# A hybrid decoder layer on one core: row statistics ahead of the first q chunk's low parts on VectorE, and the transposes of the local branch's keys one slot later

## The chip, the cores and the metric

The kernel runs on one core of one Trainium2 chip. The metric is the device time of one execution in microseconds, as a median of several runs. Beside it stands one profiled execution, whose trace gives every number of the stages below. TensorE, VectorE, ScalarE, GpSimd and SyncE (which issues most loads) each have their own queue of instructions, work through it in order, and wait for each other by semaphores.

## The reference: what is computed

One decoder layer on x of 256 rows and 1024 columns, all in float32:

```
h    = rmsnorm(x, norm1_g)
proj = h @ w_in      -> q | k,v of 3 branches | 24 branch gates | q,k,v of MoBA | 2 merge gates
y_nsa  = compressed + selected-block + sliding-window attention, gated, 8 heads in 2 key groups
y_moba = block attention, 8 heads (one block of 256 rows: causal attention)
x = x + (sig(g_A) * (y_nsa @ w_up_nsa) + sig(g_B) * (y_moba @ w_up_moba)) @ w_out
x = x + relu(rmsnorm(x, norm2_g) @ w_ff1)^2 @ w_ff2
out = rmsnorm(x, norm_f_g)
```

With 256 rows every block is selected and the window of 512 covers all rows, so the second and third branch of the first mixer are plain causal attention over their own keys. The keys of the third, the sliding window, are the "local branch's keys" of the title (`kwT` in the code). The compressed branch turns blocks of 32 keys into one each, by a small network.

## The kernel before, in words

**Two halves of a number.** TensorE multiplies in a format with fewer bits than float32, so every weight and every activation is split into a high part and a low part, and a product is three matmuls: high by high, low by high, high by low (`mm3`, lines 219 to 222). The high part of a weight chunk is a copy on ScalarE (`whi`, L106), the low part a subtraction on VectorE (`wlo`, L108); both are in `split`, which takes a chunk in two or four pieces.

**Chunks and slots.** The weights are cut into 60 chunks of mostly 1 MB, in the order of their use: kva and kvb twice in turn (chunks 0 to 3), q (4, 5), qm (6, 7), km (8, 9), vm (10, 11), then the merge gates and the later layers. `load(c)` issues the transfer of chunk c on SyncE's queue. Raw, high and low tiles have three buffers each. One chunk's matmuls are a slot. While slot c runs, ScalarE and VectorE split chunk c + 2 or so, and SyncE loads chunk c + 5, as soon as the low parts that read the same raw buffer are done.

**An order written by hand.** `at(pos, f, ...)` notes a step at a position of the slot, from 0 to 1. `run_slot` then writes the slot's matmuls one by one and puts each step in front of the first matmul whose index divided by their number is at or above its position; steps of equal position keep their order. A slot here has 24 matmuls, so 0.1 means ahead of the fourth, 0.15 ahead of the fifth. Position decides only the order in each engine's queue; when a step runs is left to the semaphores.

**The first norm.** x comes in transposed, and the projection starts on x times the norm's gain at once, without the row factor. ScalarE squares x (`row_squares`), VectorE adds the squares up (`row_sums`, L186), and `row_norm` (from line 188) finishes the statistic: four small matmuls with a tile of ones sum over the partitions into a PSUM tile, VectorE scales the result into `stat` (L192), and GpSimd raises it to the power -0.5 (`rstd`, L193) and halves it (L194). The row factor `rstd` is applied when a projection leaves PSUM, by the scale of ScalarE's copy: `evac_tm` (L275 for the compressed branch's keys and values, `kcd`; L278 for the rest). So nothing of the projection can leave PSUM before `rstd` is there.

**The compressed branch.** `cmp_gather` (L345, L353) transposes `kcd` by four matmuls for the keys and, in its second call, four for the values, and VectorE writes them into `kE`. `cmp_mlp1`, `cmp_gelu` and `cmp_mlp2` run the network; `hid` (L365) and `bdk` (L384) are its first and its last key result.

**Keys and queries.** `transp_k` (L328) transposes a tile of 128 key columns by two matmuls, and `split_evac` takes them out as a high part, the first 128 columns in float32 (ScalarE, L315, L316) and a low part (VectorE, L317). `transp_heads` (L298) does the same for four heads of a query. All these use two PSUM banks in turn, `tp` and `yb`: each new tile takes the bank of the tile before the last, and waits until that has been read. `cmp_mlp2` takes both; the bank of its first tile, which `bdk` reads, goes to the local keys, and the next but one use of it is the second call of `transp_heads` for q in slot 6.

**The steps around the change.** Slots 2 to 6 as they stand before:

```
elif c == 2:
    for k in range(2):
        at(0.9, split, 4, k, 2, "l")
    at(0.91, load, 7)
else:
    at(0.15, row_norm)
    for t in range(2):
        at(0.2, evac_tm, "kva", t, first[t], 384)
    for k in range(2):
        at(0.7, split, 5, k, 2, "h")
    at(0.82, cmp_gather, 0)
```

In slot 5 the local keys' `transp_k` stands at 0.85, behind `cmp_mlp2` at 0.6; the second q evacuation is at 1.0. In slot 6 ScalarE's high parts of chunk 8 stand at 0.0 and 0.45, VectorE's low parts of it at 0.3 and 0.46, and the two `transp_heads` of q at 0.4 and 0.5. The keys are first read in slot 9.

Of the kernel before, what the change touches and what calls it, by code (L numbers as in the profile page):

```python
# [39 lines left out]
def hybrid_layer(ctx: ExitStack, tc: tile.TileContext, gxd, w, w1c, small, const, gf, out):  # L40
# [26 lines left out]
    def acc_tile():  # L67
        return next_bank("acc")
# [130 lines left out]
    def at(pos, f, *a):  # L199
        ev.append((pos, f, a))  # L200

    def run_slot(mms):
        n = len(mms)
        es = sorted(ev, key=lambda e: e[0])
        ev.clear()
        j = 0
        for i, m in enumerate(mms):
            while j < len(es) and es[j][0] <= i / n:
                es[j][1](*es[j][2])
                j += 1  # L210
            m()
        while j < len(es):
            es[j][1](*es[j][2])
            j += 1
# [9 lines left out]
    def xstat(c, n, accs, kts):  # L224

        r = []
        h, l = hi[c], lo[c]
        order = [(t, k) for t in range(2) for k in range(4)]
        if c < 3:
            order.sort(key=lambda e: e[1])  # L230
        for t, k in order:
            kt = kts[k]
            if True:
                lh, ll = (a[:, kt, t * 128:(t + 1) * 128] for a in (hTh, hTl))
                r += mm3(accs[t][:, :n], lh, ll, h[:, k * n:(k + 1) * n],
                         l[:, k * n:(k + 1) * n], kt == 0, kt == 7)
        return r
# [11 lines left out]
    def split_events(c, hs, ls):  # L249
        for i in range(2):  # L250
            at(hs[i], split, c + 2, i, 2, "h")
        for i in range(2):
            if ls[i] <= 1:
                at(ls[i], split, c + 2, i, 2, "l")
        if ls[1] <= 1:
            at(max(ls) + 0.05, load, c + 5)

    def std_events(c):
        if 9 <= c < 20 and c % 2:
            split_events(c, (0.0, 0.06), (0.09, 0.46))  # L260
        elif 9 <= c < 20:
            split_events(c, (0.0, 0.45), (0.3, 0.8))
        else:
            split_events(c, (0.0, 0.45), (0.3, 0.46))
# [4 lines left out]
    kvb = ap_.tile([128, 2, 408], F32, name="kvb")  # L269
# [49 lines left out]
    def qk_tiles(name, n, q):  # L319
        m = 128 if q else 256  # L320
        return (ap_.tile([128, n, 128], F32, name=name + "0"),
                ap_.tile([128, n, m], F32R, name=name + "h"),
                ap_.tile([128, n, m], F32R, name=name + "l"))
# [76 lines left out]
    ksT, kwT = (qk_tiles(n, 1, False) for n in ("ks", "kw"))  # L400
# [137 lines left out]
    def unit_events(s):  # L538
        d = (s - 9) // 2
        if not 9 <= s <= 21:  # L540
            return
        if s % 2 == 0:
            at(0.1, d_norm, d)
            at(0.78, d_trans, d)
            return
        if d < 6:
            at(0.1, d_scores, d)
        if d > 0:
            at(0.1, d_pv, d - 1)
        if d < 6:  # L550
            at(0.11, d_max, d)
            at(0.2 if s > 12 else 0.5, d_exp, d, 0)
            at(0.22 if s > 12 else 0.52, d_exp, d, 1)
        if d > 0:
            at(0.12, d_yevac, d - 1)
# [17 lines left out]
    for c in range(4):  # L573
        if c == 0:
            at(0.6, load, 5)
            at(0.6, nc.sync.dma_start, w1, w1c)
        elif c == 1:
            for k in range(2):
                at(0.5, split, 3, k, 4)
            at(0.5, row_sums, 0, 4, 2)  # L580
            at(0.5, row_sums, 0, 1, 1)
            for k in range(2, 4):
                at(0.5, split, 3, k, 4)
            at(0.51, load, 6)
            for k in range(2):
                at(0.6, split, 4, k, 2, "h")
        elif c == 2:
            for k in range(2):
                at(0.9, split, 4, k, 2, "l")
            at(0.91, load, 7)  # L590
        else:
            at(0.15, row_norm)
            for t in range(2):
                at(0.2, evac_tm, "kva", t, first[t], 384)
            for k in range(2):
                at(0.7, split, 5, k, 2, "h")
            at(0.82, cmp_gather, 0)
        accs = (first, second)[c % 2]
        run_slot(xstat(c, (384, 408)[c % 2], accs, range(2 * c - 2 * (c % 2), 2 * c - 2 * (c % 2) + 4)))
    groups = [("q", C_Q, 512), ("qm", C_QM, 512), ("km", C_KM, 512), ("vm", C_VM, 512)]  # L600
    for sec, c0, n in groups:
        if sec in ("q", "qm", "km"):
            tm[sec] = ap_.tile([128, 2, 512], F32, name="qtm", bufs=2)
        if sec == "q":
            accs = [ps_e.tile([128, 512], F32, name=f"{sec}acc{t}") for t in range(2)]
        else:
            accs = [acc_tile(), acc_tile()]
        for i in range(2):
            c = c0 + i
            if c == 4:  # L610
                for t in range(2):
                    at(0.0, evac_tm, "kvb", t, second[t], 408)
                at(0.05, cmp_gather, 1)
                at(0.1, split, 5, 0, 2, "l")
                at(0.2, rope, kva, 2)
                at(0.3, split, 5, 1, 2, "l")
                at(0.35, load, 8)
                split_events(c, (0.5, 0.55), (0.8, 0.9))
                at(0.7, cmp_mlp1)
                at(0.92, cmp_gelu)  # L620
            else:
                std_events(c)
            unit_events(c)
            if c == 5:
                at(0.05, gate_evac)
                at(0.1, transp_k, kva, ksT)
                at(0.1, rope, kvb[:, :, 0:128], 2)
                at(0.6, cmp_mlp2)
                at(0.85, transp_k, kvb[:, :, 0:128], kwT)
            if c == 6:  # L630
                at(0.4, transp_heads, tm["q"], qT, 0)
                at(0.5, transp_heads, tm["q"], qT, 1)
                at(0.6, rope, tm["q"], 8)
            if c == 7:
                at(0.1, cmp_scores)
                at(0.3, cmp_softmax)
                at(0.4, transp_heads, tm["q"], qrT, 0)
                at(0.55, transp_heads, tm["q"], qrT, 1)
            if c == 8:
                at(0.35, cmp_probs_t)  # L640
                at(0.3, rope, tm["qm"], 8)
            if c == 9:
                at(0.3, transp_heads, tm["qm"], qmT, 0)
                at(0.45, transp_heads, tm["qm"], qmT, 1)
            if c == 10:
                at(0.5, rope, tm["km"], 8)
            if c == 11:
                turn["tp"] = ["tp"]
                at(0.02, transp_heads, tm["km"], kmT, 0, False)
                at(0.48, transp_heads, tm["km"], kmT, 1, False)  # L650
            if i == 1:
                at(0.5, evac_tm, sec, 0, accs[0], n)
                at(1.0, evac_tm, sec, 1, accs[1], n)
            run_slot(xstat(c, n, accs, range(4 * i, 4 * i + 4)))
# [11 lines left out]
    for g in range(4):  # L666
        accs = [acc_tile(), acc_tile()]
        for i in range(2):
            c = C_GM + 2 * g + i
# [40 lines left out]
    for sec, c0, kind, evac in (("upn", C_UPN, "n", upn_evac), ("upm", C_UPM, "m", upm_evac)):  # L710
        for i in range(2):
            c = c0 + i
# [89 lines left out]
    for i in range(4):  # L802
        c = C_WOUT + i
# [46 lines left out]
    for i in range(16):  # L850
        c = C_FF1 + i
# [177 lines left out]
```

## Time and profile before

| | |
|---|---|
| median of 3 runs | 384.33 us (384.25 to 385.54) |
| profiled execution | 383.04 us |
| its span, first to last instruction | 381.3 us |
| TensorE busy | 370.3 us (97%) |
| VectorE busy | 254.4 us (67%) |
| ScalarE busy | 205.6 us (54%) |
| GpSimd busy | 4.2 us (1%), 15 instructions |
| granted TensorE clock, mean | 0.995 |

How it is read: PE is TensorE's matmuls and PEld its weight loads, DVE is VectorE, ACT is ScalarE, POOL is GpSimd, SP is SyncE. Times in the trace are microseconds from the first instruction. L with a number is a line of the kernel. `tp<-ident,kcd` is an instruction that writes `tp` and reads `ident` and `kcd`; "x4" merges four in a row, whose sizes may differ. A bracket behind a row gives how long the engine had been idle before it and what ended that. Matmuls are pipelined and their ends are modelled, so two of them overlap in the rows, and what one costs is read from the step between starts. Times between a load's issue and its landing are in the view of the transfers. The share of TensorE is high nearly everywhere: of 40 equal slices of the span, its busy share is 80% or more in all but the last.

### The profile page before, as it was taken

What the parts mean: (1) busy time and instruction counts of PE and PEld (TensorE: products, weight loads), DVE (VectorE), ACT (ScalarE), POOL (GpSimd) and SP (SyncE); (2) the same over time, 40 slices, a digit from 0 to 9 for tenths busy, and PEclk for the clock granted to TensorE, in tenths of its full rate; (3) what the DMA queues carried; (4) which work ended last, traced back from release to release, by engine and by line L of the source; (5) the groups of instructions that cost most, each with busy time, mean ns of one, the idle gap of its engine ahead of it and who ended that gap; (6) DMA issues with size and microseconds to landing.
All of it is one profiled execution on the core that took longest, in us unless ns stands there. A gap on an engine that the chain in (4) does not pass through costs nothing.

```text
span 381.3 us, 5936 instructions
## 1 busy us (share of the span) xinstructions
PE 370.3 (97%) x2406; PEld 323.9 (85%) x2406; DVE 254.4 (67%) x397; ACT 205.6 (54%) x360; POOL 4.2 (1%) x15
## 2 busy tenths in 40 slices
PE   8989899999999999999999999999999999999993
PEld 6977778877888787778999999999998888888883
DVE  3868687897867869766868666766676254334435
ACT  5975455847747667344455646565556454433412
POOL 2000000000000000000000000000000000000000
PEclk9999999999999999999999999999999999999998
DMA  7995436332433325450675545654565545644003
GB/s 259 372 385 191 166 110 222 110 112 111 160 149 136 110 112 193 156 203 0 237 261 219 195 159 203 222 194 162 198 222 192 187 175 217 220 166 166 1 2 111
DMA packets 10972, 66.38 MB, mean 174 GB/s; under 512 B 1216, under 2 KB 2752, under 8 KB 3648
## 3 DMA queue, kind: packets, MB, share of 16 engines
q1 hardware_dynamic: 10512, 65.21, 47.0%
q10 hardware_dynamic: 432, 0.79, 0.6%
q8 instruction: 19, 0.31, 0.3%
q14 instruction: 9, 0.07, 0.1%
HBM read 64.94 MB, written 1.05 MB: 173 GB/s over the span
## 4 chain that ended last, share of the span: by engine, by line
PE 82%; DVE 6%; ACT 2%; issue 2%; POOL 0%; POOLq 0%; DVEq 0%; ACTq 0%
PE acc L217 52%; PE o L217 21%; DVE wlo L108 3%; PE yb L217 2%; ACT whi L106 1%; PE Sa L508 1%; PE Sb L508 1%; PE Sa L217 1%; PE Sb L217 1%; PE tp L298 1%; PE acc L798 0%; DVE kml L317 0%; DVE ust L472 0%; DVE kE L353 0%; PE qacc L217 0%
## 5 line engine op out<-in xcount | busy, mean ns | idle before, releaser
L106 ACT ACTIVATE whi<-raw 128x1024 fp32r<-128x1024 f32 (+2 forms) x128 | 123.4, 991 | 96.2 <-PE o L217 35.5
L108 DVE TENSOR_TENSOR wlo<-raw,whi 128x1024 fp32r<-128x1024 f32 (+2 forms) x128 | 141.5, 1138 | 44.3 <-ACT whi L106 44.2
L217 PE MATMUL acc<-h2h,whi 128*128 128x256 f32 x256 | 70.7, 276 | 0.0
L217 PE MATMUL acc<-h2l,whi 128*128 128x256 f32 x256 | 70.7, 276 | 0.0
L217 PE MATMUL acc<-h2h,wlo 128*128 128x256 f32 x256 | 70.7, 276 | 0.0
L217 PE MATMUL acc<-whi,hTh 128*128 128x512 f32 (+1 forms) x128 | 51.1, 399 | 0.4 <-ACT whi L106 0.2
L217 PE MATMUL acc<-wlo,hTh 128*128 128x512 f32 (+1 forms) x128 | 50.8, 397 | 0.3 <-DVE wlo L108 0.2
L217 PE MATMUL acc<-whi,hTl 128*128 128x512 f32 (+1 forms) x128 | 49.6, 388 | 0.0
L217 PE MATMUL o<-whi,sqh 128*128 128x512 f32 (+1 forms) x128 | 49.5, 386 | 0.0
L217 PE MATMUL o<-whi,sql 128*128 128x512 f32 (+1 forms) x128 | 49.4, 386 | 0.0
L217 PE MATMUL o<-wlo,sqh 128*128 128x512 f32 (+1 forms) x128 | 49.4, 386 | 0.0
L217 PEld LDWEIGHTS acc<-h2h,whi 128*128 128x128 f32 x256 | 48.1, 188 | 0.0
L217 PEld LDWEIGHTS acc<-h2l,whi 128*128 128x128 f32 x256 | 48.1, 188 | 0.0
L217 PEld LDWEIGHTS acc<-h2h,wlo 128*128 128x128 f32 x256 | 48.1, 188 | 0.0
L217 PEld LDWEIGHTS acc<-whi,hTh 128*128 128x128 f32 x128 | 24.3, 190 | 7.2 <-issue 1.3
L217 PEld LDWEIGHTS acc<-wlo,hTh 128*128 128x128 f32 x128 | 24.2, 189 | 5.0 <-DVE wlo L108 1.1
L217 PEld LDWEIGHTS o<-whi,sql 128*128 128x128 f32 x128 | 24.0, 188 | 4.9
L217 PEld LDWEIGHTS o<-whi,sqh 128*128 128x128 f32 x128 | 24.0, 188 | 4.8
L217 PEld LDWEIGHTS o<-wlo,sqh 128*128 128x128 f32 x128 | 24.0, 188 | 4.7
L217 PEld LDWEIGHTS acc<-whi,hTl 128*128 128x128 f32 x128 | 24.2, 189 | 4.3
L839 DVE TENSOR_TENSOR ur<-ur 128x512 f32<-128x512 f32 x16 | 11.1, 692 | 17.2 <-ACT ur L838 16.2
L841 DVE TENSOR_TENSOR sql<-ur,sqh 128x512 fp32r<-128x512 f32 x16 | 11.1, 693 | 11.2 <-ACT sqh L840 11.2
(249 smaller groups left out, 512.2 us busy)
## 6 DMA issues: line engine op xcount, KB each, us to landing
raw<-in_ff_dram SPq DMA_DIRECT2D x32, 1024.0 KB, 4.9
raw<-in_gm_dram SPq DMA_DIRECT2D x8, 1024.0 KB, 4.8
raw<-in_wout_dram SPq DMA_DIRECT2D x4, 1024.0 KB, 4.7
raw<-in_q_dram SPq DMA_DIRECT2D x2, 1024.0 KB, 6.1
raw<-in_qm_dram SPq DMA_DIRECT2D x2, 1024.0 KB, 7.2
raw<-in_km_dram SPq DMA_DIRECT2D x2, 1024.0 KB, 6.6
raw<-in_vm_dram SPq DMA_DIRECT2D x2, 1024.0 KB, 4.7
raw<-in_upn_dram SPq DMA_DIRECT2D x2, 1024.0 KB, 4.7
```

What stands on the lines that cost most here:

```text
L106: act.activation(hi[c][:, a:b], raw[c][:, a:b], AF.Copy)
L108: dve.tensor_tensor(lo[c][:, a:b], raw[c][:, a:b], hi[c][:, a:b].bitcast(F32), op=ALU.subtract)
L217: pe.matmul(o, l, r, start=start, stop=stop, skip_group_check=True)
L298: pe.transpose(tp[:, j * 256 + t * 128:j * 256 + t * 128 + 128], src[:, t, (2 * i + j) * 128:(2 * i + j + 1) * 128], ident)
L508: pe.transpose(S[x][:, j, c:c + 128], P[:, 2 * x + j, c:c + 128], ident)
L839: dve.tensor_tensor(rf, rf, rf, op=ALU.mult)
L841: dve.tensor_tensor(l, rf, h.bitcast(F32), op=ALU.subtract)
```

## The change

Two edits in the order of the steps; no instruction is added or removed.

```diff
@@ -584,12 +584,11 @@
             at(0.51, load, 6)
             for k in range(2):
                 at(0.6, split, 4, k, 2, "h")
-        elif c == 2:
+        elif c == 3:
+            at(0.1, row_norm)
             for k in range(2):
-                at(0.9, split, 4, k, 2, "l")
-            at(0.91, load, 7)
-        else:
-            at(0.15, row_norm)
+                at(0.3, split, 4, k, 2, "l")
+            at(0.31, load, 7)
             for t in range(2):
                 at(0.2, evac_tm, "kva", t, first[t], 384)
             for k in range(2):
@@ -626,8 +625,8 @@
                 at(0.1, transp_k, kva, ksT)
                 at(0.1, rope, kvb[:, :, 0:128], 2)
                 at(0.6, cmp_mlp2)
-                at(0.85, transp_k, kvb[:, :, 0:128], kwT)
             if c == 6:
+                at(0.1, transp_k, kvb[:, :, 0:128], kwT)
                 at(0.4, transp_heads, tm["q"], qT, 0)
                 at(0.5, transp_heads, tm["q"], qT, 1)
                 at(0.6, rope, tm["q"], 8)
```

The first edit moves the two low parts of chunk 4 (the first q chunk) on VectorE's queue, and the load of chunk 7 on SyncE's, from the end of slot 2 to position 0.3 of slot 3. `row_norm` goes from 0.15 to 0.1 of slot 3. On VectorE the statistic's `stat` stood behind those low parts and stands ahead of them now; on SyncE no other load lies between the old place and the new. The second edit moves the transposes of the local branch's keys, with their evacuation on ScalarE and VectorE, from three matmuls before the end of slot 5 to behind the third matmul of slot 6. On ScalarE they now stand behind the second q evacuation and the first high part of chunk 8. The order in which the two PSUM banks are taken is unchanged.

## The prediction

> **What bounds the kernel now.** I read the chain that ended last first, then TensorE's own waits, then the timeline around each of them.
>
> ```profile
> PE 82%; DVE 6%; ACT 2%; issue 2%; POOL 0%; POOLq 0%; DVEq 0%; ACTq 0%
> PE tp L345 <- ACT kcd L275: 1.2, 2, 0.7
> PE tp L328 <- DVE bdk L384: 1.0, 1, 1.0
> ```
>
> The first line is the chain by engine: TensorE's matmuls are 82% of it. The other two are TensorE's waits (us in total, times, longest). The change is aimed at exactly these two: the gather's transposes (L345), which wait for ScalarE's `kcd`, and the transposes of the local keys (L328), which wait for a PSUM bank that VectorE's `bdk` frees. A stall of TensorE taken out is worth its length, as long as nothing else is late next.
>
> **First place: what makes `kcd` late.** Start, length and instruction in order of time; a bracket gives the idle time before it and who ended it.
>
> ```profile
> 20.10 0.35 PE L217 MATMUL kvbacc<-whi,hTh 128*128 128x408 f32 x1
> 20.29 0.50 PE L217 MATMUL tp<-ones,xsq 128*128 128x2 f32 x4
> ...
> 23.52 0.35 PE L217 MATMUL kvbacc<-wlo,hTh 128*128 128x408 f32 x1
> 24.58 0.33 PE L345 MATMUL tp<-ident,kcd 128*128 128x128 f32 x1 [0.72 <-ACT kcd L275]
> 25.42 0.55 PE L345 MATMUL tp<-ident,kcd 128*128 128x128 f32 x3 [0.50 <-ACT kcd L275]
> 25.72 0.43 PE L217 MATMUL kvbacc<-whi,hTl 128*128 128x408 f32 x1
> ...
> 26.78 0.40 PE L217 MATMUL qacc<-wlo,hTh 128*128 128x512 f32 x1
> 27.02 0.60 PE L345 MATMUL tp<-ident,kcd 128*128 128x128 f32 x4
> 27.37 0.48 PE L217 MATMUL qacc<-whi,hTl 128*128 128x512 f32 x1
> ```
>
> ```profile
> 18.47 1.14 DVE L186 TENSOR_TENSOR xsq<-xsq 128x512 f32<-128x512 f32 x2
> 19.42 2.01 ACT L106 ACTIVATE whi<-raw 128x1024 fp32r<-128x1024 f32 x2 [0.84 <-DMA raw<-in_q_dram]
> 19.53 3.34 DVE L108 TENSOR_TENSOR wlo<-raw,whi 128x408 fp32r<-128x408 f32 x4
> 22.79 0.15 DVE L192 TENSOR_SCALAR stat<-tp 128x2 f32<-128x2 f32 x1
> 23.10 0.71 POOL L193 TENSOR_TENSOR rstd<-stat,mhalf 128x2 f32<-128x2 f32 x1 [20.35 <-DVE stat L192]
> 23.84 0.69 ACT L275 ACTIVATE kcd<-acc,rstd 128x512 f32<-128x512 f32 x1 [2.41 <-POOL rstd L193]
> 24.68 0.69 ACT L275 ACTIVATE kcd<-acc,rstd 128x512 f32<-128x512 f32 x1
> 26.06 3.06 DVE L353 TENSOR_TENSOR kE<-tp,sm 64x240 f32<-64x240 f32 x8 [3.11 <-issue]
> 28.36 2.04 ACT L106 ACTIVATE whi<-raw 128x1024 fp32r<-128x1024 f32 x2
> 32.15 0.22 ACT L365 ACTIVATE hid<-tp 128x64 f32<-128x64 f32 x1 [1.75 <-PE tp L217]
> ```
>
> The row sums stand in PSUM at 20.29 + 0.50 = 20.79, but `stat` starts only at 22.79, because four low parts are queued ahead of it on VectorE. Then it is a relay: `stat`, GpSimd's `rstd`, `kcd`, transposes. ScalarE sits idle for 2.41 us and VectorE for 3.11 us.
>
> **What the first edit does there.** Of the four low parts at 19.53, two belong to the second kvb chunk and stay ahead; the two of the first q chunk now come behind `stat`. A pair of 1024-column low parts takes 2.27 us (a row of the chain, below), so the first two end at 19.53 + 3.34 - 2.27 = 20.60. The statistic's matmuls move one matmul forward, from 20.29 to 20.10, and end at 20.60; their input is ready at 18.47 + 1.14 = 19.61, so TensorE doesn't wait. I put `stat` at 20.65, 2.14 earlier. With the row's spacings (23.10 - 22.79 = 0.31, then 0.71) `rstd` runs from 20.96 to 21.67. ScalarE is free at 19.42 + 2.01 = 21.43, so the two `kcd` come at 21.70 and, 0.84 later, at 22.54, and end at 23.23. TensorE reaches the transposes at 23.52 + 0.19 = 23.71 (0.19 is the step from 20.10 to 20.29): 0.48 us to spare. The second gather shows what four transposes cost without a wait: 27.37 - 27.02 = 0.35. So the next matmul starts at 24.06 and not at 25.72: **1.66 us**. The waits view's 1.2 is the low end, since a matmul's modelled end covers part of a gap; I take 1.66, from rows of the same four instructions.
>
> What else moves there: the q low parts run from 20.80 to 23.07 instead of ending at 22.87, 0.20 us later. VectorE's next work, `kE`, needs the transposes, that is 26.06 - 1.66 = 24.40, which hides it; without that cover it would cost 0.20. The load behind them on SyncE goes 0.20 later too, to 23.1:
>
> ```profile
> 20.63 2.60 SPq L90 DMA_DIRECT2D raw<-in_qm_dram  x2
> raw<-in_qm_dram SPq DMA_DIRECT2D x1, 1024.0 KB, 7.1
> ```
>
> The first row is both qm loads, the second the landing time of the earlier. At 7.1 us the later one lands near 30.2; ScalarE takes it up only behind `hid`, at 32.15 - 1.66 = 30.49, so this costs nothing. The earlier one lands at 20.63 + 7.1 = 27.73. ScalarE, 2.14 us ahead, is ready for its high parts at 28.36 - 2.14 = 26.22, waits for the data, and is done at 27.73 + 2.04 = 29.77. That is 0.7 us before `hid` needs ScalarE. So the transfer takes ScalarE's extra lead, not TensorE's.
>
> **Second place.** From the second gather on, the chain goes over VectorE and ScalarE to `bdk`. Its rows (start, length, what), then TensorE, VectorE and ScalarE around the transposes:
>
> ```profile
> 27.18 0.45 PE tp L345 x4
> ...
> 31.42 3.49 DVE wlo L108 x3
> ...
> 38.98 2.27 DVE wlo L108 x2
> 41.24 0.11 DVE bdk L384
> ```
>
> ```profile
> 39.97 0.40 PE L217 MATMUL qacc<-whi,hTl 128*128 128x512 f32 x1
> 41.40 0.44 PE L328 MATMUL tp<-ident,kvb 128*128 128x128 f32 x2 [1.03 <-DVE bdk L384]
> 41.59 0.47 PE L217 MATMUL qacc<-whi,hTh 128*128 128x512 f32 x1
> 41.88 0.39 ACT L315 ACTIVATE kwh<-tp 128x256 fp32r<-128x256 f32 x1 [2.96 <-PE tp L328]
> 42.46 0.42 DVE L317 TENSOR_TENSOR kwl<-tp,kwh 128x256 fp32r<-128x256 f32 x1
> 42.57 0.69 ACT L278 ACTIVATE qtm<-qacc,rstd 128x512 f32<-128x512 f32 x1
> 43.16 1.05 ACT L106 ACTIVATE whi<-raw 128x1024 fp32r<-128x1024 f32 x1
> ```
>
> All of this hangs on the gather's transposes, so it comes 1.66 us earlier as a whole, and the stall would be there again, no longer and no shorter. The second edit puts six matmuls (three left of slot 5, three of slot 6) ahead of the transposes: at a step of 27.02 - 26.78 = 0.24 that is 1.4 us of other work. Unstalled, TensorE would be there at 39.97 + 0.24 = 40.21 in the old time, with the six at 41.6; the bank is free at 41.40. So the stall goes, with 0.2 us to spare: 1.03 by the row, 41.40 - 40.21 = 1.19 by the step; I take **1.15**.
>
> The price is a later bank for the q heads' second transposes, which take the same one. ScalarE now has the q evacuation and one high part of 1.05 us ahead of `kwh`. With both gains in, the keys' transposes start at 39.93, slot 5's last matmul, four steps before them, ends near 39.4, the evacuation (43.16 - 42.57 = 0.59) is over near 40.0, the high part at 41.05, `kwl` near 42.0; TensorE asks for the bank nine matmuls and six transposes later, near 42.55. Half a microsecond is left, so I cost it at nothing; any lateness above that goes to TensorE. Matmuls, transposes and DMAs are moved, and none is added.
>
> **Sum.** 1.66 + 1.15 = 2.8 us, against the profiled execution's 383.04 (span 381.3 and 1.7 around it). The median of the runs is 384.33, 1.29 above; the gains are stalls and carry over: 384.33 - 2.8 = **381.5**. Behind 42 us every load, high part and low part is released by these engines, so the rest moves forward as a whole. With the low ends (1.2 and 1.03) it is 382.1.
>
> **Rivals.** *GpSimd is held by the low parts.* This is the one I take most seriously. In the trace of before, GpSimd's power never runs beside VectorE: VectorE idles from 22.94 to 26.06, and at the end it waits for the power too.
>
> ```profile
> 371.31 0.56 POOL L905 TENSOR_TENSOR fst<-fst,mhalf 128x1 f32<-128x1 f32 x1 [347.20 <-DVE fst L901]
> 371.91 0.75 DVE L912 TENSOR_SCALAR gx<-gx,fst 128x384 f32<-128x384 f32 x2 [0.73 <-POOL fst L905]
> ```
>
> After the change a q low part starts right behind `stat`, and `rstd` would run beside it. If it has to wait for the end of the part under way (20.80 + 1.13 = 21.93), it ends at 22.64, the second `kcd` ends at 22.67 + 0.84 + 0.69 = 24.20, and the transposes that stood at 25.42 come at 24.25: 1.17 instead of 1.66, sum 2.3, **382.0**. If it waits for both parts (23.07), `rstd` ends at 23.78, as before: only the 1.15 stays, **383.2**. Nothing in the trace decides it, for or against. The Trainium skill ("SBUF — State Buffer", section "Who interferes with whom") speaks for it: a VectorE instruction with two SBUF inputs and a GpSimd instruction that reads SBUF contend for one lock, and the second to issue blocks until the first ends. No run here shows the two together; by that rule the time is one of these two, 382.0 or 383.2.
>
> *The second stall only moves.* If the q-head transposes find their bank taken, or `bdk` doesn't come forward with TensorE (its spare time is 0.2 us), TensorE waits there instead, up to the whole 1.15: **382.7**. For it: the thin margins. Against: each row that sets them hangs on the same transposes.
>
> *Slower: ScalarE blocked by a load.* The high part now ahead of `kwh` reads the first km chunk.
>
> ```profile
> 32.66 2.60 SPq L90 DMA_DIRECT2D raw<-in_km_dram  x2
> raw<-in_km_dram SPq DMA_DIRECT2D x1, 1024.0 KB, 6.4
> raw<-in_kva_dram SPq DMA_DIRECT2D x1, 768.0 KB, 8.4
> ```
>
> It lands at 32.66 - 1.66 + 6.4 = 37.4, 2.6 us before ScalarE is there at 40.0. Each microsecond that it lands after 40.0 + 0.55 holds the bank and TensorE for one; the time is worse than before only from 40.55 + 2.8 = 43.4 on, a landing of 12.4 us where the longest here is 8.4. At 13.5 us: **385.4**.
>
> *It doesn't do what it says.* If `stat` starts no earlier, because its input and not the queue makes it late, the first gain is gone: 383.2. The row sums are in PSUM at 20.79, so I don't believe it.
>
> **How the numbers follow.** Forecast 0.45; `rstd` held by one part 0.25, by both 0.13; the second stall moves 0.10; slower 0.04; no effect of the first edit 0.03. About 0.5%, 1.9 us, can be told from no change, so the line is at 382.4. Faster are the forecast, nearly all of the one-part case and the lesser forms of a moved stall: 0.45 + 0.17 + 0.02 = 0.64. Slower by over 0.5% is 0.04, within it the rest, 0.32. The range goes up to 383.3, which takes in both parts held (383.2) and the moved stall, and down to 380.9: the full gain, less half of the 1.3 us by which the runs before differ (384.25 to 385.54).
>
> **What would show it.** Right: `stat` near 20.7, `rstd` near 21.0 and no longer than 0.71, `kcd` near 21.7, no wait at L345, the matmul behind it at 24.1; no wait at L328 and the keys' transposes near 39.9. Wrong: `rstd` starting or ending at the end of a low part; a wait of TensorE at the q-head transposes; ScalarE waiting for raw data past 27.8 us or ahead of `kwh`; or the gain there at 42 us and gone at 100, which would mean that something behind is bound by the loads and not by TensorE.

## The result, and the profile after

The changed kernel takes 381.38 us (median of 19 runs), the kernel before 384.15 us (19 runs beside them): a ratio of 0.9929, with a 95% interval of 0.9904 to 0.9954. That is 2.77 us less, where 2.8 were forecast (381.5). Some runs of most kernels here, of these two as well, are 2 to 6 us longer than the rest, which widens the intervals; four of the profiles below are of such runs, and each loses 4.1 us between 170 and 300 us, away from the stages read here. The sum came out, but one of its two terms did not, and the profile shows which.

The profiled execution took 381.45 us, 1.6 less than that of before. It started worse: the first matmul of slot 3 is at 20.51 and no longer at 19.55, because the first weights landed late. From that matmul to the last of the kernel it is 2.55 us shorter, which is the number to hold against the sum. Before, then after, first and last of these matmuls:

```profile
19.55 0.34 PE L217 MATMUL kvbacc<-whi,hTh 128*128 128x408 f32 x1
...
374.74 0.28 PE L217 MATMUL yb<-whi,sql 128*128 128x256 f32 x1
```

```profile
20.51 0.34 PE L217 MATMUL kvbacc<-whi,hTh 128*128 128x408 f32 x1
...
373.15 0.28 PE L217 MATMUL yb<-whi,sql 128*128 128x256 f32 x1
```

374.74 - 19.55 = 355.19; 373.15 - 20.51 = 352.64. The chain that ended last and the longest of TensorE's waits, after:

```profile
PE 88%; DVE 4%; ACT 2%; issue 2%; DMA 1%; POOL 1%; SPq 1%; POOLq 0%; DVEq 0%; ACTq 0%
```

```profile
PE acc L217 <- ACT whi L106: 1.5, 2, 0.9
```

TensorE's share of the chain went from 82% to 88%. The waits at L345 and L328 are no longer in the list; the 1.5 us at its head are the late first weights. But a list of waits is not the whole of a stall, as the first place shows. The first matmul of slot 4 before, which ends the stretch that is compared here, then TensorE in the first place after:

```profile
26.55 0.40 PE L217 MATMUL qacc<-whi,hTh 128*128 128x512 f32 x1
```

```profile
21.06 0.50 PE L217 MATMUL tp<-ones,xsq 128*128 128x2 f32 x4
...
24.50 0.35 PE L217 MATMUL kvbacc<-wlo,hTh 128*128 128x408 f32 x1
24.69 0.94 PE L345 MATMUL tp<-ident,kcd 128*128 128x128 f32 x4
25.39 0.43 PE L217 MATMUL kvbacc<-whi,hTl 128*128 128x408 f32 x1
...
26.21 0.40 PE L217 MATMUL qacc<-whi,hTh 128*128 128x512 f32 x1
```

The four transposes take 25.39 - 24.69 = 0.70 from their start to the start of the next matmul; in the second gather they take 0.35 before and 0.36 after. So some 0.35 us of the stall are left, inside a row that shows no wait. Slot 3, from its first matmul to the first of slot 4, took 26.55 - 19.55 = 7.00 us and takes 26.21 - 20.51 = **5.70**: 1.30 gained and not 1.66. The relay that feeds it, after:

```profile
20.48 1.07 DVE L108 TENSOR_TENSOR wlo<-raw,whi 128x408 fp32r<-128x408 f32 x2
21.60 0.16 DVE L192 TENSOR_SCALAR stat<-tp 128x2 f32<-128x2 f32 x1
21.68 2.36 DVE L108 TENSOR_TENSOR wlo<-raw,whi 128x1024 fp32r<-128x1024 f32 x2
21.91 1.56 POOL L193 TENSOR_TENSOR rstd<-stat,mhalf 128x2 f32<-128x2 f32 x1 [19.16 <-DVE stat L192]
23.51 0.69 ACT L275 ACTIVATE kcd<-acc,rstd 128x512 f32<-128x512 f32 x1 [1.57 <-POOL rstd L193]
24.34 0.69 ACT L275 ACTIVATE kcd<-acc,rstd 128x512 f32<-128x512 f32 x1
29.98 2.01 ACT L106 ACTIVATE whi<-raw 128x1024 fp32r<-128x1024 f32 x2 [1.81 <-DMA raw<-in_qm_dram]
31.89 0.20 ACT L365 ACTIVATE hid<-tp 128x64 f32<-128x64 f32 x1
```

`stat` now comes right behind the kvb low parts, as forecast. But `rstd` takes **1.56 us, where it took 0.71**. The last two rows are the transfer that takes ScalarE's lead: it waits 1.81 us for qm data, and `hid` stands right behind the high parts. The second place: the matmul of before that ends the stretch compared there, then the place after (bank freed by `bdk`, keys' transposes, their evacuation, and the q-head transposes that take the bank next):

```profile
44.44 0.40 PE L217 MATMUL acc<-whi,hTh 128*128 128x512 f32 x1
```

```profile
39.63 0.39 PE L217 MATMUL qacc<-whi,hTl 128*128 128x512 f32 x1
40.83 0.18 DVE L384 TENSOR_TENSOR bdk<-tp,kc 128x32 f32<-128x32 f32 x1
41.23 0.38 PE L328 MATMUL tp<-ident,kvb 128*128 128x128 f32 x2
41.33 1.05 ACT L106 ACTIVATE whi<-raw 128x1024 fp32r<-128x1024 f32 x1
42.28 0.37 ACT L315 ACTIVATE kwh<-tp 128x256 fp32r<-128x256 f32 x1
42.84 0.39 PE L217 MATMUL acc<-whi,hTh 128*128 128x512 f32 x1
42.85 0.42 DVE L317 TENSOR_TENSOR kwl<-tp,kwh 128x256 fp32r<-128x256 f32 x1 [0.81 <-ACT kw L316]
43.97 0.60 PE L298 MATMUL tp<-ident,qtm 128*128 128x128 f32 x4
```

No wait is left. From the matmul at 39.63 (the 21st of slot 5) to the one at 42.84 (the tenth of slot 6), both transposes' places inside, it is 3.21 us; before it was 4.47 (39.97 to 44.44): **1.26** gained. 1.30 and 1.26 make 2.56, and 2.55 arrive at the last matmul, so nothing behind gives any of it back.

### The profile page after: what moved, and what is told of

It is laid out like the page before. It is cut to its first block, busy times and chain, and to the rows that moved or that the text cites. A ratio compares the mean times of both kernels' runs of the same rounds, so it can differ in the third digit from the quotient of the medians.

```text
span 379.7 us, 5935 instructions
## 1 busy us (share of the span) xinstructions
PE 369.5 (97%) x2406; PEld 323.6 (85%) x2406; DVE 254.5 (67%) x397; ACT 205.5 (54%) x360; POOL 5.4 (1%) x15
## 4 chain that ended last, share of the span: by engine, by line
PE 88%; DVE 4%; ACT 2%; issue 2%; DMA 1%; POOL 1%; SPq 1%; POOLq 0%; DVEq 0%; ACTq 0%
PE acc L217 53%; PE o L217 22%; PE qacc L217 3%; PE yb L217 2%; PE kvbacc L217 2%; DMA raw<-in_kva_dram 1%; DVE wlo L108 1%; ACT whi L106 1%; PE Sb L508 1%; PE Sa L508 1%; PE Sa L217 1%; PE tp L217 1%; PE Sb L217 1%; PE tp L298 1%; POOL rstd L193 0%
```

## The experiments

The theory after this profile: two separate stalls; the first is only partly gone because the low part that now runs beside `rstd` holds GpSimd until it ends. Ratios are to the kernel before, run beside each. They are worked out from the single runs and are not quotients of the two medians, so the longer runs can move them: for the one-piece kernel below the medians alone would give 0.9928, and the ratio is 0.9957. "The stretch" is slot 3 as above, 7.00 before and 5.70 after.

**The first edit alone.** The local keys' transposes go back to slot 5:

```diff
+                at(0.85, transp_k, kvb[:, :, 0:128], kwT)
             if c == 6:
-                at(0.1, transp_k, kvb[:, :, 0:128], kwT)
```

> Only the first edit; the local keys' transposes stay in slot 5. Measured from the first kvbacc matmul of slot 3 to the first qacc matmul of slot 4, the kernel before takes 7.00 us and the changed one 5.70. Theory (two separate stalls, the first only partly removed because the low part holds GpSimd): 5.7 here too, rstd near 1.56 us long, and the wait of the keys' transposes for bdk there again with 1.0 us; the time 1.3 us below before, ratio 0.9966. Rival (the second stall was a consequence of the first and goes with it): no wait at the keys' transposes, ratio near 0.993. Rival (the first edit brings nothing, the gain is the second's): ratio 1.000.

It took 382.74 us beside 383.82: 0.9963 (0.9949 to 0.9977). TensorE's waits and GpSimd's row:

```profile
PE tp L328 <- DVE bdk L384: 1.0, 1, 1.0
PE tp L345 <- ACT kcd L275: 0.3, 1, 0.3
```

```profile
21.22 1.54 POOL L193 TENSOR_TENSOR rstd<-stat,mhalf 128x2 f32<-128x2 f32 x1 [18.47 <-DVE stat L192]
```

The wait for `bdk` is there again in full, so it was no consequence of the first stall. `rstd` is long again. The stretch is 5.96 (19.55 to 25.51), 0.26 more than expected: `stat` itself came 1.37 us behind the slot's first matmul (20.92 - 19.55), where it comes 1.09 behind it in the changed kernel (21.60 - 20.51), and all that follows came as much later.

**The second edit alone.** The keys' transposes move to 0.1 of slot 6; the first q chunk's low parts stay ahead of the statistic.

> Only the second edit; low parts of the first q chunk ahead of the statistic as before. Theory: the stretch of slot 3 stays 7.0 us, rstd 0.71 us long with VectorE idle beside it, no wait at the keys' transposes; the stretch from the matmul ahead of their old place (whi,hTl, the eighteenth of slot 5 before the merge) to the tenth of slot 6 falls from 4.47 to 3.2 us; the time 1.25 us below before, ratio 0.9967. Rival (the stall only moves to the q-head transposes): a wait of about 1 us there, ratio 1.000.

382.87 us beside 383.82: 0.9977 (0.9942 to 1.0011). The interval includes no change; the stages decide. TensorE's wait and GpSimd's row:

```profile
PE tp L345 <- ACT kcd L275: 1.6, 2, 1.1
```

```profile
23.63 0.71 POOL L193 TENSOR_TENSOR rstd<-stat,mhalf 128x2 f32<-128x2 f32 x1 [20.87 <-DVE stat L192]
```

The second place takes 3.21 us (40.51 to 43.72), exactly as with both edits. (The expectation counts its first matmul as the eighteenth of slot 5; it is the 21st, the one at 39.97 before.) No wait is at L328 or L298, so the stall doesn't move. `rstd` is 0.71 with VectorE idle. The stretch came out longer than expected, 7.34 and not 7.0, since the low parts ahead of `stat` had to wait 0.27 us for their high parts in this execution.

**How long GpSimd is held.** Six kernels change only what VectorE runs right behind `stat`. First, the low parts in four pieces:

```diff
-            for k in range(2):
-                at(0.3, split, 4, k, 2, "l")
+            for k in range(4):
+                at(0.3, split, 4, k, 4, "l")
```

> The changed kernel with the q chunk's low parts behind the statistic in four pieces of 512 columns and not two of 1024. Theory (GpSimd's rstd waits for the end of the one low part that is running, then runs its normal way): the running piece ends 0.57 us earlier than the 1024-column one, so rstd takes 0.9 to 1.0 us and not 1.56, both kcd are ready before TensorE asks, the stretch of slot 3 falls from 5.70 to 5.2 to 5.3 us, the time 0.4 us below the changed kernel, ratio to before 0.992. Rival (rstd is slowed all the while VectorE works beside it, whatever the pieces): rstd stays near 1.56 and the stretch near 5.7. Rival (the longer rstd has nothing to do with VectorE): the same.

380.91 us beside 383.82: 0.9925 (0.9899 to 0.9952). Second, in one piece (`at(0.3, split, 4, 0, 1, "l")`):

> The changed kernel with the q chunk's low part behind the statistic in one piece of 2048 columns, some 2.2 us long. Theory (rstd waits for the end of the instruction that is running): rstd takes near 2.6 us, kcd comes 1.0 us later than in the changed kernel, the stretch of slot 3 is near 6.7 us, the time near 1.0 us above the changed kernel, ratio to before 0.996. Rival (slowed all the while VectorE works beside it, or nothing to do with VectorE): rstd 1.56, stretch 5.7, ratio 0.993.

381.05 us beside 383.82: 0.9957 (0.9925 to 0.9988). Third, an instruction ahead of the low parts that reads one SBUF tile (`hi[3]`), and fourth, one that reads two over the same columns:

```diff
+    def filler():
+        dve.tensor_reduce(st4_all[:, 64:65], hi[3][:, 0:1632].bitcast(F32), op=ALU.max, axis=AX)
...
+            at(0.3, filler)
             for k in range(2):
                 at(0.3, split, 4, k, 2, "l")
```

```diff
+    def filler():
+        dve.tensor_tensor(xsq.rearrange("p k q -> p (k q)")[:, 0:1632], hi[3][:, 0:1632].bitcast(F32),
+                          lo[3][:, 0:1632].bitcast(F32), op=ALU.max)
```

> The changed kernel with one more VectorE instruction between stat and the q chunk's low parts: a maximum over 1632 columns of one tile in SBUF, some 1.8 us long, whose result nobody reads. VectorE is then as busy beside rstd as in the changed kernel, but with an instruction of one SBUF input. Theory (rstd waits only for a VectorE instruction with two SBUF inputs that is under way): rstd 0.71 us, no wait at the gather's transposes, the stretch from the first kvbacc matmul of slot 3 to the first qacc matmul of slot 4 near 5.35. Rival (any VectorE instruction under way holds rstd): rstd near 2.1 and the stretch near 6.3. The filler pushes the low parts back by 1.8 us, to the gather's results, so the time is about that of the changed kernel, ratio to before near 0.993.

> The same, but the filler is an elementwise maximum of two SBUF tiles over the same 1632 columns. Theory (rstd waits to the end of the two-input instruction under way, then takes 0.6 us): rstd near 2.1 us, ending 0.6 us later than in the changed kernel, the stretch near 6.3, the time 0.6 to 0.9 us above the changed kernel, ratio 0.995. Rival (a slowdown that doesn't depend on the length of the instruction): rstd near 1.55, the stretch 5.7.

These two fillers differ in their operation too, a reduction against an elementwise one. So the elementwise one was run with one of its inputs in PSUM, first the kva sums, then the statistic's own four columns (`tp` of `row_norm`, kept as `U["rn"]`) read over and over:

```diff
+        v = lambda a: a[:, 0:1536].rearrange("p (a d) -> p a d", d=4)
+        dve.tensor_tensor(v(xsq.rearrange("p k q -> p (k q)")),
+                          U["rn"][:, None, 0:4].to_broadcast([128, 384, 4]),
+                          v(hi[3]).bitcast(F32), op=ALU.max)
```

> The filler as an elementwise maximum again, over 1536 columns, but with one tile from SBUF and the other from PSUM (the kva sums, read four times over); some 1.7 us long. It has the operation of the two-input filler and the SBUF reads of the one-input filler. Theory (two SBUF inputs hold rstd): rstd 0.71 us, the stretch near 5.35. Rival (it is the operation, an elementwise one against a reduction, and not where its inputs are): rstd near 2.0, the stretch near 6.2.

> The elementwise filler with one input from SBUF and one from PSUM once more, now with the statistic's own four columns in PSUM, read 384 times over, so that nothing but stat is ahead of it; 1536 columns, 1.7 us or longer, beside rstd from its start. Theory (two SBUF inputs hold rstd): rstd 0.71 us, the stretch near 5.35. Rival (it is the elementwise operation, not where its inputs are): rstd near 2.0 or longer, the stretch 6.2 or longer.

381.02 us beside 383.72 with one input: 0.9925 (0.9902 to 0.9947). 381.90 beside 383.72 with two: 0.9951 (0.9930 to 0.9971). With PSUM, one run each: 382.01 us with the kva sums, beside 383.43, and 380.25 with the statistic's columns, beside 384.37; for single runs the rows say more. The kva sums missed their purpose: that filler was queued behind ScalarE's evacuations of the same sums, started at 22.57, when `rstd` (20.85 to 21.56) was over, and says nothing. The instruction behind `stat` and `rstd`, in this order: four pieces, one piece, the reduction of one input, the elementwise filler with two SBUF inputs, and that with the statistic's columns in PSUM.

```profile
21.17 0.69 DVE L108 TENSOR_TENSOR wlo<-raw,whi 128x512 fp32r<-128x512 f32 x1
...
21.41 1.03 POOL L193 TENSOR_TENSOR rstd<-stat,mhalf 128x2 f32<-128x2 f32 x1 [18.65 <-DVE stat L192]
```

```profile
22.55 2.29 DVE L108 TENSOR_TENSOR wlo<-raw,whi 128x2048 fp32r<-128x2048 f32 x1 [1.11 <-ACT whi L106]
...
21.59 0.71 POOL L193 TENSOR_TENSOR rstd<-stat,mhalf 128x2 f32<-128x2 f32 x1 [18.84 <-DVE stat L192]
```

```profile
23.24 1.84 DVE L405 TENSOR_REDUCE st<-whi 128x1 f32<-128x1632 f32 x1
...
23.48 0.71 POOL L193 TENSOR_TENSOR rstd<-stat,mhalf 128x2 f32<-128x2 f32 x1 [20.73 <-DVE stat L192]
```

```profile
20.80 1.85 DVE L405 TENSOR_TENSOR xsq<-whi,wlo 128x1632 f32<-128x1632 f32 x1
...
21.04 2.18 POOL L193 TENSOR_TENSOR rstd<-stat,mhalf 128x2 f32<-128x2 f32 x1 [18.29 <-DVE stat L192]
```

```profile
20.87 1.75 DVE L406 TENSOR_TENSOR xsq<-tp,whi 128x1536 f32<-128x1536 f32 x1
...
21.11 0.71 POOL L193 TENSOR_TENSOR rstd<-stat,mhalf 128x2 f32<-128x2 f32 x1 [18.36 <-DVE stat L192]
```

The last three settle it: the same place, nearly the same length (1.84, 1.85 and 1.75 us), and `rstd` is 0.71 beside one SBUF input, whether the instruction reduces or works by elements, and 2.18 beside two. The length of the two-input instruction sets how long:

| behind `stat` | it ends at | `rstd` ends at | later by | `rstd` takes | stretch |
|---|---|---|---|---|---|
| two inputs, 512 columns | 21.86 | 22.44 | 0.58 | 1.03 | 5.36 |
| two inputs, 1024 columns (the change) | 22.91 | 23.47 | 0.56 | 1.56 | 5.70 |
| two inputs, 1632 columns | 22.65 | 23.22 | 0.57 | 2.18 | 6.32 |
| one input, reduction, 1632 columns | 25.08 | 24.19 | no hold | 0.71 | 5.35 |
| one input and PSUM, 1536 columns | 22.62 | 21.82 | no hold | 0.71 | 5.36 |

The 1024-column row is the first of the two low parts, which starts at 21.68 and takes 1.23. GpSimd waits for the end of the instruction under way, and only for that one: the next low part is queued right behind, and `rstd` ends while it runs. In the changed kernel the two low parts and GpSimd's next step, the halving (0.22 us in the kernel before):

```profile
21.68 1.23 DVE L108 TENSOR_TENSOR wlo<-raw,whi 128x1024 fp32r<-128x1024 f32 x1
...
22.82 1.22 DVE L108 TENSOR_TENSOR wlo<-raw,whi 128x1024 fp32r<-128x1024 f32 x1
...
23.56 0.55 POOL L194 TENSOR_SCALAR stat<-rstd 128x2 f32<-128x2 f32 x1
```

The halving starts while the second low part is under way, and is held to its end in turn: 24.11, against 24.04. The second low part itself is not slowed by `rstd`, which is still running when it starts. The one-piece kernel missed its expectation for a reason of its own: a whole low part needs both high parts, the second came late, VectorE stood idle, and `rstd` ran free at 0.71, ahead of the low part, with a stretch of 5.35. So it tells nothing about length; it is one more case in which an idle VectorE leaves `rstd` at 0.71.

**The margins of the second edit.** The keys' transposes three matmuls earlier (`at(0.0, ...)` of slot 6), and seven later (`at(0.38, ...)`):

> The changed kernel with the local keys' transposes three matmuls earlier, at 0.0 of slot 6. In the changed kernel they start at 41.23 and bdk ends at 41.01, so there are some 0.2 us to spare. Theory (the bank that bdk frees sets the earliest place): TensorE gets there 0.69 us earlier and waits about 0.5 us; the time 0.5 us above the changed kernel, ratio near 0.994. Rival (bdk comes forward with TensorE or the wait is not for it): no wait, ratio 0.993.

> The changed kernel with the local keys' transposes seven matmuls later, right ahead of the q heads' transposes in slot 6. In the changed kernel the evacuation of the keys' bank ends at 43.27 and TensorE asks for that bank at 43.97, 0.7 us to spare. Theory (the stall can move to the q-head transposes): the keys' transposes at 42.8 in that profile's time, kwh 0.4, kw 0.3, kwl 0.4 behind them, the bank free near 44.2 with TensorE there near 43.95; a wait of 0.2 to 0.5 us at the second q-head transposes, ratio near 0.994. Rival (the margin is larger than the rows show): no wait, ratio 0.993.

381.85 us beside 383.72 with the earlier place (0.9962; 0.9935 to 0.9989) and 381.49 with the later (0.9954; 0.9937 to 0.9971). The transposes that wait, earlier and later:

```profile
41.31 0.44 PE L328 MATMUL tp<-ident,kvb 128*128 128x128 f32 x2 [0.36 <-DVE bdk L384]
```

```profile
43.40 0.66 PE L298 MATMUL tp<-ident,qtm 128*128 128x128 f32 x4 [0.20 <-DVE kwl L317]
```

Both waits are at the places that the prediction named: for `bdk`, 0.36 us as shown and 0.51 by the step (41.31 - 40.57 - 0.23); for `kwl` at the second q-head transposes, 0.20 as shown and 0.36 by the step (43.40 - 42.81 - 0.23). The first has the size of its margin, 0.69 - 0.22 = 0.47. The second is smaller than 1.6 - 0.70 = 0.9, because ScalarE has its high part behind it by then and `kwh` waits for TensorE alone (0.85 us idle in that run). The place that the change takes lies in a window between the two; from these waits and a step of 0.23, an estimate is that it could lie five matmuls later without a wait, and one earlier with a wait of about 0.05 us. Slot 3 is that of the change in both kernels, and its stretch is 5.70 and 5.71 again.

**The version with four pieces against the change**, side by side:

> The changed kernel once more, beside the next one on the same chip. Theory: ratio to before 0.993, 2.6 to 2.8 us below it; rstd 1.56 us, stretch from the first kvbacc matmul of slot 3 to the first qacc matmul of slot 4 of 5.7 us.

> The changed kernel with the q chunk's low parts in four pieces, measured closely. Theory (what is left of the first stall, 0.35 us, goes, since the running instruction that holds rstd is shorter): rstd 1.03 us, stretch 5.36, the time 0.3 to 0.4 us below the changed kernel beside it, ratio to before 0.992. Rival (the two more instructions on VectorE eat it up): the same time as the changed kernel.

The change took 381.30 us (0.9907; 0.9875 to 0.9939), the four pieces 380.99 (0.9924; 0.9890 to 0.9957), both beside 384.24. The medians say 0.31 us less for the four pieces, the ratios say the opposite, and the intervals overlap: the times don't order them. The stages do: 5.93 against 5.36. GpSimd's rows and, for the change, the low parts:

```profile
21.84 2.36 DVE L108 TENSOR_TENSOR wlo<-raw,whi 128x1024 fp32r<-128x1024 f32 x2
...
21.84 1.79 POOL L193 TENSOR_TENSOR rstd<-stat,mhalf 128x2 f32<-128x2 f32 x1 [19.09 <-DVE stat L192]
```

```profile
22.44 1.03 POOL L193 TENSOR_TENSOR rstd<-stat,mhalf 128x2 f32<-128x2 f32 x1 [19.68 <-DVE stat L192]
```

In this execution of the change the low part began as late as `rstd` itself, and `rstd` took 1.79: held to 21.84 + 1.23 = 23.07, and ended 0.56 later. That is the rule of the table again, in a case not made for it. It is also why the stretch here is 5.93 and not 5.70, so a part of the 0.57 between the two kernels belongs to this execution; against the 5.70 of the first profile of the change it is 0.34.

Whether the stages' gains arrive at the end can be read from more than one pair of profiles. From the first matmul of slot 3 to the last of the kernel it is 355.19 us before, 354.09 with the first edit alone, 354.32 with the second alone, 352.64 and 352.89 in the two profiles of the change, and 352.29 here with four pieces. Each differs from before by the sum of its two places' gains to within 0.05 us.

## Why the prediction was right, and where it was wrong

**The forecast of 381.5 (measured 381.38) and faster:** right, and the mechanism of both gains, a stall of TensorE taken out, was right. The equality is partly luck: the first term was too large by 0.36, the second too small by 0.11, and the medians moved 0.2 more than the profiles did (2.77 and 2.55).

**"With the row's spacings `rstd` runs from 20.96 to 21.67":** the step that failed. The row of 0.71 was taken from a place where VectorE idles, and put into a place where it doesn't. `stat` itself came as worked out (right behind the two kvb low parts). `rstd` took 1.56, both `kcd` came 0.85 later for that, the 0.48 us to spare was used up, and 0.35 us of the stall stayed. The first term measured 1.30 and not 1.66.

**What the working had right there:** in the kernels whose `rstd` isn't held the stretch is 5.35 to 5.37, a gain of 1.63 to 1.65, and with four pieces 5.36. So the 1.66 is the size of the whole stall, and the 0.71 is the figure of this sum that failed.

**The rival "held by one part":** right in its mechanism. It had `rstd` ending 0.71 behind the low part; it ends 0.57 behind it, hence 1.30 where the rival said 1.17. "Held by both parts" fell: `rstd` ends while the second low part runs. By the Trainium skill ("SBUF — State Buffer", section "Who interferes with whom") a VectorE instruction with two SBUF inputs and a GpSimd instruction that reads SBUF contend for an exclusive lock, and a VectorE instruction with at most one SBUF input, outside its 2-port modes, doesn't contend. The runs agree on GpSimd's side, with 2.18 against 0.71 us; that VectorE is held in turn they don't show, since the low part that starts beside the running `rstd` takes 1.22 us, and the one before it 1.23. Held by one part had a chance of 0.25 in the prediction and held by both 0.13, 0.38 together beside the forecast's 0.45.

**"It comes 1.66 us earlier as a whole, and the stall would be there again":** right but for the size. With the first edit alone the wait for `bdk` is 1.0, as before.

**The second term, 1.15:** measured 1.26 with both edits, and the same stretch of 3.21 with the second alone. The upper of its two ends (1.19) was the better one. Gaps that are read off the step between starts were nearer than the waits shown, here and, where `rstd` isn't held, in the first place too (1.66 against 1.2).

**The margins:** 0.2 us at `bdk` and half a microsecond at the q-head transposes were forecast. The rows show 41.23 - 41.01 = 0.22 and 43.97 - 43.27 = 0.70, and moving the step by three matmuls one way (0.7 us) or seven the other (1.6 us) brings out a wait.

**What hides the rest:** the 0.20 us on the q low parts is hidden in front of `kE`, which VectorE reaches after 1.69 us idle. The transfer of qm takes ScalarE's lead, as worked out. It landed later than I had it, and high parts and `hid` stand without a gap, so the 0.7 us to spare there were gone in this execution, yet the next matmul in the queue was not late for it. The rivals "the second stall only moves" and "slower" did not occur.

## What to carry to other kernels

A duration from the profile holds in the surroundings it was taken in: ask what else ran when it was measured, and what will run beside it after the change. Here a tiny GpSimd step in a relay was held to the end of the VectorE instruction with two SBUF inputs that was under way, however short the step itself; put a short instruction behind the step that feeds it, or one with a single SBUF input, or cut the long one up. And a step may be moved out of a stall into a window: reckon its two ends, what frees its buffer and who takes the buffer next, and put it between them.

## What the runs showed of the hardware that was not expected

`rstd` of 128x2 elements took 0.71 us beside an idle VectorE or one that reads only one tile from SBUF, and 1.03, 1.56 and 2.18 us when a two-input instruction of 512, 1024 or 1632 columns was under way; it ended 0.56 to 0.58 us behind that instruction each time. The halving behind it (L194) went from 0.22 to 0.55 to 0.62 us in the same way, and ended 0.07 to 0.08 us behind the low part under way. The other direction was not seen: two low parts of 1024 columns take 2.36 us beside `rstd` and 2.35 without it.
